# Expert weights' parts 2 and 3 read during the mixer's last chunk, into a buffer shared by both phases

## The chip, the core and the metric

The kernel runs on one core of a Trainium2 chip. The metric is the device time of one execution in microseconds (us). The engines are named as in the profile: PE (TensorE matmuls), PEld (its weight loads), DVE (VectorE), ACT (ScalarE), POOL (GpSimd) and SP (SyncE). SPq, ACTq and POOLq are the queues from which these engines issue DMA transfers.

## What is computed

One layer over 2048 tokens of width 1024: a mixer of three parallel branches with an output projection, then a mixture of 16 experts (4 groups of 4, two experts per token), then a final norm, all in float32.

```python
def reference(x, ...):
    mix = hybrid_mixer(h, ...)                  # z = rmsnorm(x) @ W_in, branches A, B, C, then @ w_out
    h = h + mix
    ffn = hierarchical_moe(rms_norm(h, norm_ffn_g[l]), ...)
    h = h + ffn
    return rms_norm(h, final_norm_g)

def expert_block(args):                         # inside hierarchical_moe, for a block of sorted tokens
    xb, e = args
    return (jax.nn.silu(xb @ w_gate[e]) * (xb @ w_up[e])) @ w_down[e]
```

## The kernel before

**First phase (`phases12`).** The mixer's projections are cut into 22 chunks of weight columns, 14 of `w_in` and 8 of `w_out`, numbered n = 0 to 21. Generators that run a step per tick of a small scheduler (`Flow`) read a chunk's float32 weights, split them on ACT and DVE into a high and a low part, and keep them in a tile `w`. The pool of that tile has two buffers, used in turn, so chunk n takes the buffer of chunk n-2. The last loop goes over `h` (two halves of 1024 tokens), `m` (four chunks of `w_out`) and `t` (eight tiles of 128 tokens). With `m == 3` each finished tile is written to two DRAM tensors, `hd` and `hc`, and squared on ACT for the norm. A generator `route` then selects experts, sorts the tokens and writes tables; between its halves it reads the first two parts of the experts' weights into two buffers `stg` of the pool `c8`.

**Second phase (`moe`).** The experts' weights come in 96 parts of 1 MB, six an expert: u = 0 to 3 are gate and up columns, u = 4 and 5 are rows of the down projection. Part n is read by two DMAs of 512 KB into a staging place `raw(n)`, and DVE splits it into the ring slot n % 9: first the high half (L1600, or L1598 for a down part), then the low half (L1618, L1616). ACT does some of the splitting of parts 0 and 1. DVE counts finished parts in the semaphore `s_w`. Parts 0 and 1 are staged in the two `stg` buffers, parts 2 to 5 in ring slots that are still unused (6 and 7), and from part 6 on the two `stg` buffers are used in turn: SP issues part n (n > 7) only when part n-2 has been split (L1567). The slots are reused when PE has done the last block of the expert that they held.

PE takes blocks of 128 tokens, sorted by expert. For block b it does the gate and up products in two halves of two groups of 12 or more matmuls (`gu`, L1692), each group waiting for its part by `s_w`, and the down product of the block before (`down`, L1731 to L1733). ACT applies the activation (`glu`), POOL multiplies (`hm`), gathers tokens, scatters results back, and scales finished rows by the final norm's gains `gf`.

What the steps touch, in lines that words don't say:

```python
                    for n in range(NST, 96):
                        if n == 4:
                            sp.wait_ge(p_q, 2)
                        if n >= 6:
                            sp.wait_ge(s_w, n - NST + 1 if n > 7 else n - 5)
...
        raw = lambda n: ring[:, 6 + (n - 2) // 2, n % 2].bitcast(F32) if 2 <= n < 6 else stg[n % NST]
```

Of the kernel before, what the change touches and what calls it, by code (L numbers as in the profile page):

```python
# [9 lines left out]
F32 = mybir.dt.float32  # L10
F32R = mybir.dt.float32r
BF = mybir.dt.bfloat16
I32 = mybir.dt.int32
# [4 lines left out]
DRAM = bass.MemoryType.DRAM  # L18

P = 128  # L20
S = 2048
D = 1024
# [74 lines left out]
NST = 2  # L97
# [44 lines left out]
        self.until(lambda: not self.g)  # L142


def phases12(tc, io, hd, hc, tab, gcol, ident, c8, stg):


    nc = tc.nc
# [2 lines left out]
    with ctx:  # L151
# [3 lines left out]
        lg = tab[:, 0:320].rearrange("p (t n) -> p t n", n=20)  # L155
        base = pool("base")
        small = pool("small", 2)
        wp = pool("w", 2)
        rawp = pool("raw", 2)
        uvp = pool("uvp")  # L160
        psz = pool("psz", 4, space=PSUM)
# [39 lines left out]
        def wgen():  # L201
            for n in range(len(chunks)):
                raws = load_w_raw(n)
                yield
                while begun[0] < n - 1:
                    yield
                w = wp.tile([P, 2, 8, 276], F32R, name="w")
                for k in range(0, 8, 2):
                    rw_ = raws[k // 4][:, k % 4:k % 4 + 2, :]
                    for j in range(2):  # L210
                        g = col(chunks[n][2], k + j)
                        A.activation(w[:, 0, k + j, 0:256], rw_[:, j], AF.Copy, scale=g)  # L212
                    for j in range(2):
                        stt(w[:, 1, k + j, 0:256], rw_[:, j], col(chunks[n][2], k + j), w[:, 0, k + j, 0:256].bitcast(F32), OP.mult, OP.subtract)
                    yield
                if n in routed:
                    while "rw" not in done:
                        yield
                    G.tensor_copy(w[:, 0, :, 256:276], routed[n])
                    tt(w[:, 1, :, 256:276], routed[n], w[:, 0, :, 256:276].bitcast(F32), OP.subtract, G)  # L220
                wt[n] = w
                if 6 <= n < 14:
                    yield from route_w(n - 6)
                if n == 2:
                    yield from spatial_w()
            done.add("w")
# [859 lines left out]
        def route():  # L1086
# [237 lines left out]
            for k in range(2):  # L1324
                G.iota(digit[:, k], pattern=[[1, 16], [0, 48]], base=1 + 32 * k, channel_multiplier=0, allow_small_or_imprecise_dtypes=True)
            digits(slice(0, 8))
            while stg is not None and len(stg) < NST:
                t = c8.tile([P, 2048], F32, name="stg", tag="c8")
                for o, i in stage(io, t, len(stg)):
                    nc.sync.dma_start(out=o, in_=i)  # L1330
                stg.append(t)
            yield from half(1)

            acc = bank(psm, "m")[:, 0:96]
# [105 lines left out]
        for h in range(2):  # L1440
            F.until(lambda: ("r", h) in done)
            for m in range(4):
                w = chunk(n)
                n += 1
                if h == 0 and m == 1:
                    F.add(pipeline([(lambda p=p: yprep(p), lambda: ("a", 1) in done) for p in range(4, 8)]))
                for t in range(8):
                    F.until(lambda: ("y", h * 8 + t) in done and h * 8 + t in ht)
                    N = 276 if m == 3 else 256
                    za, zc = bank(psz, "z"), bank(psz, "z")  # L1450
                    dst = [za[:, 0:N], (bank(psm, "m")[:, 0:N] if m == 3 else za[:, 256:512]), zc[:, 0:N]]
                    for j, ks in enumerate(((0, 1, 2), (3, 4, 5), (6, 7))):
                        for k in ks:
                            split3(nc, dst[j], [xT[:, s, k, t * P:(t + 1) * P] for s in range(2)],
                                   [w[:, s, k, 0:N] for s in range(2)], k == ks[0], k == ks[-1])
                    x = ht[h * 8 + t][:, m * 256:(m + 1) * 256]
                    for j in range(3):
                        r = rsd[:, j, h * 8 + t:h * 8 + t + 1]
                        stt(x, dst[j][:, 0:256], r, x, OP.mult, OP.add)
                        if m == 3:  # L1460
                            l = lg[:, h * 8 + t, :]
                            stt(l, dst[j][:, 256:276], r, l, OP.mult, OP.add)
                    F.tick()
                    g = h * 8 + t
                    whole = g < 12
                    if m == 2 and not whole:
                        p2_sq(g, (0, 768), False)
                        if t == 7:
                            ts(hss[3][:, 0], hss[3][:, 0], 1.0 / D, EPS, OP.mult, OP.add)
                    if m == 3:  # L1470
                        p2_sq(g, (0 if whole else 768, D), True)
                        if t % 4 == 3 or h == 1 and t == 1:
                            F.add(p2_post(list(range(g - (1 if h == 1 and t < 4 else 3), g + 1)), whole))
                        done.add(("yfree", 8 + t))
# [20 lines left out]
def moe(tc, io, hd, hc, out, tab, gcol, ident, stg):  # L1495
# [5 lines left out]
    with ctx:  # L1501
        E = ctx.enter_context
        mp = E(tc.tile_pool(name="moe", bufs=1))
        pp = E(tc.tile_pool(name="mps", bufs=1, space=PSUM))
        ring = mp.tile([P, RING, 2, 2048], F32R, name="ring")
        xg = mp.tile([P, 2, D + 16], F32, name="xg")
        sc = mp.tile([P, 48, 2], F32, name="sc")
        xs = mp.tile([P, 2, 2, 8, P], F32R, name="xs")
        hs = mp.tile([P, 512], F32, name="hs")
        hu = mp.tile([P, 512], F32, name="hu")  # L1510
        hh = mp.tile([P, 2, 4, P], F32R, name="hh")
        yb = mp.tile([P, 2, D], F32, name="yb")
        gf = mp.tile([P, D], F32, name="gf")
        idf = mp.tile([P, 48], I32, name="idf")
        nw = mp.tile([P, 12], F32, name="nw")
        jb = hu[:, 0:256].bitcast(mybir.dt.float8e4)
        nid = mp.tile([P, P], F32R, name="nid")
        s0, vh, nt, c15, gl, ceps, cmag = (nw[:, i:i + 1] for i in range(7))
        ya = nw[:, 8:10]
        ew = mp.tile([P, 6, 2], F32, name="ew")  # L1520
        es, et, ev, ey = ew[:, 0:2], ew[:, 2], ew[:, 3], ew[:, 4:6]
        pg = [pp.tile([P, 512], F32, name="pg%d" % i) for i in range(2)]
        pt = [pp.tile([P, 4, P], F32, name="pt%d" % i) for i in range(2)]
# [3 lines left out]
        S_ = lambda n: tc.alloc_semaphore(n)  # L1527
        s_st = [S_("st%d" % i) for i in range(NST)]
        s_w, s_hi, s_ha, p_q, p_c = S_("w"), S_("hi"), S_("ha"), S_("pq"), S_("pc")
        s_er = [S_("er%d" % i) for i in range(4)]  # L1530

        raw = lambda n: ring[:, 6 + (n - 2) // 2, n % 2].bitcast(F32) if 2 <= n < 6 else stg[n % NST]
        s_u = [S_("u%d" % i) for i in range(6)]
        s_hm, s_hT, s_T, s_hlo, s_d0 = (S_(n) for n in ("hm", "hT", "T", "hlo", "d0"))
        s_Tl, s_hl, a_xh, a_hh, a_sc, p_k = (S_(n) for n in ("Tl", "hl", "axh", "ahh", "asc", "pk"))
# [22 lines left out]
        with tc.tile_critical():  # L1558
            with nc.Block() as blk:
                @blk.sync  # L1560
                def _(sp):
                    sp.wait_ge(p_q, 1)
                    for n in range(NST, 96):
                        if n == 4:
                            sp.wait_ge(p_q, 2)
                        if n >= 6:
                            sp.wait_ge(s_w, n - NST + 1 if n > 7 else n - 5)  # L1567
                        if n == RING:
                            sp.dma_start(out=gf, in_=io["final_norm_g"].unsqueeze(0).to_broadcast((P, D))).then_inc(s_gf, 16)
                        for o, i in stage(io, raw(n), n):  # L1570
                            sp.dma_start(out=o, in_=i).then_inc(s_er[n - 2] if n < 6 else s_st[n % NST], 16)

                @blk.vector
                def _(v):
                    nhi = nha = 0
                    for n in range(96):
# [4 lines left out]
                            v.wait_ge(s_u[u], c)  # L1581
                        if n >= 6:
                            v.wait_ge(s_st[j], 32 * ((n - 6) // NST + 1))
                        elif n >= NST:
                            v.wait_ge(s_er[n - 2], 32)
                        src = raw(n)
                        r = n % RING
                        q = n % 6
# [191 lines left out]
                def _(a):  # L1780
# [28 lines left out]
                    def glu(b, f):  # L1809
                        a.wait_ge(s_u[2 * f + 1], b + 1)  # L1810
                        if f == 0:
                            a.wait_ge(a_sc, 2 * b + 2)
                        a.activation(hs[:, f * 256:(f + 1) * 256], pg[f][:, 0:256], AF.Silu, scale=sc[:, b, 0:1])
                        a.activation(hu[:, f * 256:(f + 1) * 256], pg[f][:, 256:512], AF.Copy, scale=sc[:, b, 0:1]).then_inc(a_g[f], 1)  # L1814

# [57 lines left out]
                    evx(0)  # L1873
                    scale(0)
                    evxl(0)
                    if 3 in AH:
                        a.wait_ge(s_er[1], 32)
                        hi(3, range(4))
                    chain(a, nb, 0, NBMAX, step)
                    n = 0  # L1880
                    for i in (1, 0):
# [81 lines left out]

def trunk(tc, io, out):
    nc = tc.nc
    with tc.tile_pool(name="outer", bufs=1) as po, tc.tile_pool(name="c8", bufs=2) as c8, tc.tile_pool(name="odr", bufs=1, space=DRAM) as pd:
        tab = po.tile([P, 368], F32, name="tab")
        gcol = po.tile([P, 8], F32, name="gcol")
        ident = po.tile([P, P], F32, name="ident")
        make_identity(nc, ident)  # L1970
        hd = pd.tile([S + P, D], F32, name="hd")
        hc = pd.tile([S, D + 16], F32, name="hc")
        stg = []
        phases12(tc, io, hd, hc, tab, gcol, ident, c8, stg)
        moe(tc, io, hd, hc, out, tab, gcol, ident, stg)


# [23 lines left out]
```

## Time and profile before

| | before |
|---|---|
| median of 3 runs | 1590.1 us (1586.15 to 1593.86) |
| the profiled execution, its time | 1590.12 us |
| its span, first to last instruction | 1588.3 us |
| mean granted TensorE clock | 0.966 |
| PE busy | 94% |
| DVE, ACT, POOL busy | 61%, 54%, 31% |
| HBM | 217.09 MB read, 76.94 MB written |

The share of busy time is a mean over the whole span. The first phase ends and the second begins at about 762 us; what one stage is limited by has to be read in that stage. Times in the rows below are counted from the span's start.

### The profile page before, as it was taken

To read this page: it belongs to the slowest core of one execution; us is meant where nothing else is said; L and a number is where in the kernel's file an instruction comes from. 1 tells how busy PE (TensorE), PEld (TensorE's weight loads), DVE (VectorE), ACT (ScalarE), POOL (GpSimd) and SP (SyncE) were. 2 spreads that over 40 slices of the span, in tenths; PEclk is the share of its full clock that TensorE was granted. 3 is DMA by queue.
4 is the path that set the end of the run, shared out by engine and by line. 5 is a ranking of instruction groups with operands and counts; after the bars stand their busy time and mean duration, and the time that the engine had idled before them with its cause. 6 is when DMAs were issued, how large, how long until landed. Compare 5 with 4: busy or idle time off the path is not lost.

```text
span 1588.3 us, 25588 instructions
## 1 busy us (share of the span) xinstructions
PE 1489.4 (94%) x8373; PEld 1283.5 (81%) x8374; DVE 976.4 (61%) x2009; ACT 865.6 (54%) x1915; POOL 484.6 (31%) x400
## 2 busy tenths in 40 slices
PE   7998989999999999996899899999999999999993
PEld 6776888878899989996688678888888888888882
DVE  6588752664642678888888876577888858203001
ACT  6368544687454444311346456665666665666662
POOL 0132000000000000010355545655555555455442
PEclk9999988999999999998899999999999999999996
DMA  6247733213633627607678887778888877434342
GB/s 179 69 80 142 208 104 120 93 54 93 188 99 104 236 81 263 241 27 267 215 226 241 259 253 198 214 214 264 272 222 236 261 220 204 126 75 107 90 116 74
DMA packets 212862, 267.46 MB, mean 168 GB/s; under 512 B 34808, under 2 KB 177344, under 8 KB 212736
## 3 DMA queue, kind: packets, MB, share of 16 engines
q1 hardware_dynamic: 187792, 201.95, 40.3%
q0 software_dynamic: 24672, 62.80, 16.3%
q8 instruction: 78, 1.28, 0.3%
q10 hardware_dynamic: 272, 1.05, 0.2%
q14 instruction: 48, 0.39, 0.1%
HBM read 217.09 MB, written 76.94 MB: 185 GB/s over the span
## 4 chain that ended last, share of the span: by engine, by line
PE 74%; DVE 13%; DMA 4%; ACT 4%; issue 2%; POOL 1%; SPq 0%; DVEq 0%; POOLq 0%; ACTq 0%
PE pg L1692 24%; PE z L90 8%; PE z L92 8%; PE z L91 8%; PE pd L1733 4%; PE pd L1732 4%; PE pd L1731 4%; DMA stg<-in_expert_w_up_dram 3%; DVE ring L1600 2%; PE pt L1699 2%; DVE ring L1618 2%; DVE ht L171 1%; DVE w L171 1%; PE m L924 1%; DVE xT L169 1%
## 5 line engine op out<-in xcount | busy, mean ns | idle before, releaser
L1692 PE MATMUL pg<-ring,xs 128*128 x2016 | 488.3, 395 | 9.7 <-DVE ring L1618 8.0
L1692 PEld LDWEIGHTS pg<-ring,xs 128*128 128x128 f32 x2016 | 378.2, 189 | 89.7 <-issue 11.8
L90 PE MATMUL z<-w,xT 128*128 128x256 f32 (+1 forms) x848 | 250.4, 295 | 5.6 <-DVE ht L171 3.8
L92 PE MATMUL z<-w,xT 128*128 128x256 f32 (+1 forms) x848 | 244.9, 289 | 6.9 <-DVE xT L169 6.9
L91 PE MATMUL z<-w,xT 128*128 128x256 f32 (+1 forms) x848 | 244.6, 288 | 0.0
L1600 DVE TENSOR_SCALAR ring<-stg,gcol 128x512 fp32r<-128x512 f32 x242 | 130.9, 602 | 169.8 <-PE pg L1692 86.7
L1618 DVE SCALAR_TENSOR_TENSOR ring<-stg,gcol,ring 128x512 fp32r<-128x512 f32 x248 | 213.9, 923 | 0.0
L90 PEld LDWEIGHTS z<-w,xT 128*128 128x128 f32 x848 | 164.3, 194 | 9.0 <-issue 5.1
L92 PEld LDWEIGHTS z<-w,xT 128*128 128x128 f32 x848 | 164.1, 194 | 8.2 <-DVE xT L169 8.2
L91 PEld LDWEIGHTS z<-w,xT 128*128 128x128 f32 x848 | 164.5, 194 | 1.4 <-issue 1.4
L1731 PE MATMUL pd<-ring,hh 128*128 x336 | 131.4, 391 | 1.7 <-DVE hh L1637 1.7
L1896 POOL DMA_INDIRECT hd<-yb,tab x41 | 77.5, 1891 | 177.8 <-ACT yb L1835 177.8
L1733 PE MATMUL pd<-ring,hh 128*128 x336 | 131.2, 390 | 0.0
L1732 PE MATMUL pd<-ring,hh 128*128 x336 | 131.2, 390 | 0.0
L1910 POOL TENSOR_TENSOR hs<-hs,hu 128x256 f32<-128x256 f32 x84 | 106.5, 1268 | 50.1 <-ACT hu L1814 47.8
L1945 POOL TENSOR_TENSOR yb<-yb,gf 128x1024 f32<-128x1024 f32 x40 | 116.2, 2905 | 4.7 <-ACT hu L1860 4.7
L171 DVE SCALAR_TENSOR_TENSOR w<-raw,vec,w 128x256 fp32r<-128x256 f32 x176 | 82.0, 510 | 55.4 <-ACT w L212 55.4
L212 ACT ACTIVATE w<-raw,vec 128x256 fp32r<-128x256 f32 x176 | 77.1, 497 | 60.8 <-PE z L92 36.7
L90 PE MATMUL z<-xT,w 128*128 128x512 f32 x256 | 109.8, 429 | 0.2 <-ACT xT L312 0.2
L171 DVE SCALAR_TENSOR_TENSOR ht<-z,rsd,ht 128x256 f32<-128x256 f32 x176 | 85.1, 484 | 30.1 <-PE z L92 22.2
L91 PE MATMUL z<-xT,w 128*128 128x512 f32 x256 | 101.5, 396 | 0.2 <-DVE xT L169 0.2
L92 PE MATMUL z<-xT,w 128*128 128x512 f32 x256 | 101.3, 396 | 0.0
(441 smaller groups left out, 2573.2 us busy)
## 6 DMA issues: line engine op xcount, KB each, us to landing
stg<-in_expert_w_gate_dram SPq DMA_DIRECT2D x62, 512.0 KB
stg<-in_expert_w_up_dram SPq DMA_DIRECT2D x62, 512.0 KB
stg<-in_expert_w_down_dram SPq DMA_DIRECT2D x60, 512.0 KB
raw<-in_w_in_dram SPq DMA_DIRECT2D x48, 256.0 KB
raw<-in_w_out_dram SPq DMA_DIRECT2D x24, 512.0 KB
ht<-in_x_dram SPq DMA_DIRECT2D x16, 512.0 KB
yp<-yTd SPq DMA_DIRECT2D x8, 1024.0 KB
hd<-ht SPq DMA_DIRECT2D x16, 512.0 KB
```

Source lines behind the costliest of these rows:

```text
L90: nc.tensor.matmul(ps, ah, bh, start=first, stop=False)
L91: nc.tensor.matmul(ps, ah, bl, start=False, stop=False)
L92: nc.tensor.matmul(ps, al, bh, start=False, stop=last)
L171: stt = lambda o, a, s, b, o0, o1: V.scalar_tensor_tensor(out=o, in0=a, scalar=s, in1=b, op0=o0, op1=o1)
L1600: x = v.tensor_scalar(out=ring[:, r, 0, sl], in0=src[:, sl], scalar1=g, scalar2=None, op0=OP.mult)
L1618: x = v.scalar_tensor_tensor(out=ring[:, r, 1, sl], in0=src[:, sl], scalar=g, in1=hi, op0=OP.mult, op1=OP.subtract)
L1692: i = t.matmul(pg[f], xx[j // 2], w[j % 2], start=k == 0 and j == 0, stop=k == 7 and j == 2)
L1731: t.matmul(pd[n], hh[:, 0, kf], w[0], start=kf == 0, stop=False)
L1732: t.matmul(pd[n], hh[:, 0, kf], w[1], start=False, stop=False)
L1733: i = t.matmul(pd[n], hh[:, 1, kf], w[0], start=False, stop=kf == 3)
L1910: g.tensor_tensor(out=o, in0=o, in1=hu[:, f * 256:(f + 1) * 256], op=OP.mult).then_inc(s_hm, 1)
L1945: g.tensor_tensor(out=z, in0=z, in1=gf, op=OP.mult).then_inc(p_z, 1)
```

## The change

Chunks with an even n take their `w` tile from a new pool `we` of one buffer, which both phases see; odd chunks take it from the old pool, which now has one buffer. Chunk 20 is the last in `we`. When chunk 21 begins (`h == 1`, `m == 3`), ACT issues the reads of parts 2 and 3 into that buffer (`early`). In the second phase parts 4 and 5 alone are staged in the ring (slot 7), and SP issues them without the wait for `p_q` 2. Several small tiles of the second phase (`yb`, `gf`, `hs`, `hu`, `sc`, `idf`, `nw`, `ew`) are now cuts of `early`: `yb`, `gf`, `hs` and `hu` lie where parts 2 and 3 are staged, the others behind them. Before its first write of `hs`, ACT waits until four parts have been split. A branch that was never taken (`3 in AH`) is removed.

```diff
-                w = wp.tile([P, 2, 8, 276], F32R, name="w")
+                w = (wp if n % 2 else we).tile([P, 2, 8, 276], F32R, name="w")
...
-            while stg is not None and len(stg) < NST:
+            for n in range(NST):
                 t = c8.tile([P, 2048], F32, name="stg", tag="c8")
...
+                if h == 1 and m == 3:
+
+                    t = we.tile([P, 4416], F32, name="w", tag="w")
+                    for j in range(2):
+                        for o, i in stage(io, t[:, j * 2048:(j + 1) * 2048], 2 + j):
+                            A.dma_start(out=o, in_=i)
+                    stg.append(t)
...
+        early = stg[NST]
...
+        yb = cut(2 * D).rearrange("p (a n) -> p a n", a=2)
+        gf = cut(D)
+        hs, hu = cut(512), cut(512)
...
+        raw = lambda n: early[:, (n - 2) * 2048:(n - 1) * 2048] if 2 <= n < 4 else ring[:, 7, n % 2].bitcast(F32) if 4 <= n < 6 else stg[n % NST]
...
                     sp.wait_ge(p_q, 1)
-                    for n in range(NST, 96):
-                        if n == 4:
-                            sp.wait_ge(p_q, 2)
+                    for n in range(4, 96):
                         if n >= 6:
                             sp.wait_ge(s_w, n - NST + 1 if n > 7 else n - 5)
...
+                        if b == 0 and f == 0:
+                            a.wait_ge(s_w, 4)
```

On ACT the four reads stand in the first phase between the squares of chunk 20's last four tiles (128x768) and those of chunk 21's first four (128x1024); this is the piece of the difference there:

```order
 L212 ACTIVATE w<-raw,vec 128x256 x8
 L1065 ACTIVATE junk,hss<-ht 128x768 x4
+L1450 DMA w<-in_expert_w_gate_dram 128x4x256
+L1450 DMA w<-in_expert_w_up_dram 128x4x256
+L1450 DMA w<-in_expert_w_gate_dram 128x4x256
+L1450 DMA w<-in_expert_w_up_dram 128x4x256
 L1065 ACTIVATE junk,hss<-ht 128x1024 x4
 L1065 ACTIVATE junk,hss<-ht 128x256 x4
```

Nothing else moves on ACT there; the squares stand behind four issues more.

On SP the second phase began with parts 2 and 3 (gate, up), then parts 4 and 5 (down) behind a second wait for `pq`, then part 6 behind `w`, the count of split parts (the kernel before):

```order
L1571 DMA ring<-in_expert_w_gate_dram 128x4x256 [waits pq]
L1571 DMA ring<-in_expert_w_up_dram 128x4x256
L1571 DMA ring<-in_expert_w_gate_dram 128x4x256
L1571 DMA ring<-in_expert_w_up_dram 128x4x256
L1571 DMA ring<-in_expert_w_down_dram 128x1024 [waits pq]
L1571 DMA ring<-in_expert_w_down_dram 128x1024 x3
L1571 DMA stg<-in_expert_w_gate_dram 128x4x256 [waits w]
L1571 DMA stg<-in_expert_w_up_dram 128x4x256
```

The changed kernel begins there with the down parts:

```order
L1582 DMA ring<-in_expert_w_down_dram 128x1024 [waits pq]
L1582 DMA ring<-in_expert_w_down_dram 128x1024 x3
L1582 DMA stg<-in_expert_w_gate_dram 128x4x256 [waits w]
L1582 DMA stg<-in_expert_w_up_dram 128x4x256
L1582 DMA stg<-in_expert_w_gate_dram 128x4x256 [waits w]
```

Four reads have gone from the queue's head, and every part behind them stands two parts earlier.

On DVE the start of the second phase was this (before; `er0` and `er1` are the arrivals of parts 2 and 3, `er2` that of part 4):

```order
L1618 SCALAR_TENSOR_TENSOR ring<-stg,gcol,ring 128x512 [waits ha] x6
L1600 TENSOR_SCALAR ring<-ring,gcol 128x512 [waits er0]
L1600 TENSOR_SCALAR ring<-ring,gcol 128x512 x3
L1618 SCALAR_TENSOR_TENSOR ring<-ring,gcol 128x512 [waits hi] x4
L1600 TENSOR_SCALAR ring<-ring,gcol 128x512 [waits er1]
L1600 TENSOR_SCALAR ring<-ring,gcol 128x512 x3
L1618 SCALAR_TENSOR_TENSOR ring<-ring,gcol 128x512 [waits hi] x4
L1598 CAST ring<-ring 128x1024 [waits er2]
```

In the changed kernel (`w` is the shared buffer, and `er0` is now part 4):

```order
L1629 SCALAR_TENSOR_TENSOR ring<-stg,gcol,ring 128x512 [waits ha] x6
L1611 TENSOR_SCALAR ring<-w,gcol 128x512 x4
L1629 SCALAR_TENSOR_TENSOR ring<-w,gcol,ring 128x512 [waits hi] x4
L1611 TENSOR_SCALAR ring<-w,gcol 128x512 x4
L1629 SCALAR_TENSOR_TENSOR ring<-w,gcol,ring 128x512 [waits hi] x4
L1609 CAST ring<-ring 128x1024 [waits er0]
```

The waits for the arrival of parts 2 and 3 are gone from DVE; the operations and their order are the same.

## Rows read from the trace of the kernel before

**Rows 1.** Chain that ended last, 760 to 1000 us: start, length, what.
```profile
765.29 7.77 DMA ring<-in_expert_w_up_dram
773.08 1.67 DVE ring L1600 x4
...
920.39 3.03 PE pg L1692 x12
```

**Rows 2.** PE's waits, 760 us to the end: total us, times, longest.
```profile
PE pg L1692 <- DVE ring L1618: 8.0, 3, 4.1
```

**Rows 3.** PE's waits, 921 us to the end, the whole list.
```profile
PE ph L1699 <- issue: 3.4, 1, 3.4
PE pd L1731 <- DVE hh L1637: 1.7, 1, 1.7
```

**Rows 4.** Timeline of PE: start, length, what, and in brackets idle before.
```profile
879.94 5.61 PE L1692 MATMUL pg<-ring,xs 128*128 x24
...
890.14 2.88 PE L1692 MATMUL pg<-ring,xs 128*128 x12
...
898.08 0.39 PE L1733 MATMUL pd<-ring,hh 128*128 x1
902.52 4.60 PE L1692 MATMUL pg<-ring,xs 128*128 x12 [4.05 <-DVE ring L1618]
909.22 4.60 PE L1692 MATMUL pg<-ring,xs 128*128 x12 [2.09 <-DVE ring L1618]
...
920.39 3.03 PE L1692 MATMUL pg<-ring,xs 128*128 x12 [1.84 <-DVE ring L1618]
```

**Rows 5.** Windows: PE, PEld, DVE, ACT, POOL busy, PE clock, DMA share, GB/s.
```profile
902.40:907.00 4.60, 4.48 (x12) 3.31 (x12) 2.94 (x6) 4.16 (x11) 2.37 (x1) 0.63 1.03 252
```

**Rows 6.** Timeline of DVE.
```profile
722.74 0.16 DVE L170 TENSOR_SCALAR hss<-hss 128x2 f32<-128x2 f32 x1
...
763.62 5.44 DVE L1618 SCALAR_TENSOR_TENSOR ring<-stg,gcol,ring 128x512 fp32r<-128x512 f32 x8
773.08 1.67 DVE L1600 TENSOR_SCALAR ring<-ring,gcol 128x512 fp32r<-128x512 f32 x4 [4.02 <-DMA ring<-in_expert_w_up_dram]
...
786.24 2.35 DVE L1616 TENSOR_TENSOR ring<-ring 128x1024 fp32r<-128x1024 f32 x2
...
806.87 5.30 DVE L1600 TENSOR_SCALAR ring<-stg,gcol 128x512 fp32r<-128x512 f32 x4 [2.09 <-DMA stg<-in_expert_w_up_dram]
```

**Rows 7.** DVE's waits for staged parts, 760 to 921 us; none names a ring slot.
```profile
DVE ring L1600 <- DMA stg<-in_expert_w_up_dram: 18.5, 12, 2.7
DVE ring L1598 <- DMA stg<-in_expert_w_down_dram: 4.2, 3, 1.5
```

**Rows 8.** Timeline of POOL.
```profile
807.29 3.42 POOL L1930 TENSOR_SCALAR gf<-gf 128x1024 f32<-128x1024 f32 x1
...
826.03 2.95 POOL L1945 TENSOR_TENSOR yb<-yb,gf 128x1024 f32<-128x1024 f32 x1
```

**Rows 9.** Timeline of SP's queue: DMA issues.
```profile
764.85 0.39 SPq L1571 DMA_DIRECT2D ring<-in_expert_w_gate_dram  x1
...
772.75 1.77 SPq L1571 DMA_DIRECT2D ring<-in_expert_w_down_dram  x4
...
775.84 3.14 SPq L1571 DMA_DIRECT2D stg<-in_expert_w_gate_dram  x1
...
794.30 0.37 SPq L1571 DMA_DIRECT2D stg<-in_expert_w_gate_dram  x1
```

**Rows 10.** Timeline of ACT.
```profile
716.83 1.06 ACT L1065 ACTIVATE junk<-ht 128x1024 bf16<-128x1024 f32 x1 [1.86 <-DVE ht L171]
...
781.47 0.48 ACT L1813 ACTIVATE hs<-pg,sc 128x256 f32<-128x256 f32 x1
```

**Rows 11.** Timeline of ACT's queue, its one DMA issue.
```profile
28.89 0.45 ACTq L318 DMA_DIRECT2D xp<-in_x_dram  x1
```

**Rows 12.** Windows, columns as in rows 5.
```profile
748.00:752.00 4.00, 0.46 (x3) 0.08 (x2) 3.63 (x18) 0.21 (x1) 1.59 (x5) 0.50 0.01 3
```

More of the change, by code (lines that the diff above doesn't have):

```diff
@@ L142, in drain, with phases12 @@
         self.until(lambda: not self.g)
-def phases12(tc, io, hd, hc, tab, gcol, ident, c8, stg):
+def phases12(tc, io, hd, hc, tab, gcol, ident, c8, we, stg):
     nc = tc.nc
@@ L157, in phases12 @@
         small = pool("small", 2)
-        wp = pool("w", 2)
+        wp = pool("w")
         rawp = pool("raw", 2)
@@ L1326, in route @@
             digits(slice(0, 8))
-            while stg is not None and len(stg) < NST:
+            for n in range(NST):
                 t = c8.tile([P, 2048], F32, name="stg", tag="c8")
-                for o, i in stage(io, t, len(stg)):
+                for o, i in stage(io, t, n):
                     nc.sync.dma_start(out=o, in_=i)
-                stg.append(t)
+                stg.insert(n, t)
             yield from half(1)
@@ L1505, in moe, with cut @@
         ring = mp.tile([P, RING, 2, 2048], F32R, name="ring")
+        early = stg[NST]
+        off = [0]
+        def cut(n):
+            off[0] += n
+            return early[:, off[0] - n:off[0]]
         xg = mp.tile([P, 2, D + 16], F32, name="xg")
-        sc = mp.tile([P, 48, 2], F32, name="sc")
         xs = mp.tile([P, 2, 2, 8, P], F32R, name="xs")
-        hs = mp.tile([P, 512], F32, name="hs")
-        hu = mp.tile([P, 512], F32, name="hu")
+        yb = cut(2 * D).rearrange("p (a n) -> p a n", a=2)
+        gf = cut(D)
+        hs, hu = cut(512), cut(512)
         hh = mp.tile([P, 2, 4, P], F32R, name="hh")
[L1512 to L1515, printed above, removed]
+        sc = cut(96).rearrange("p (b j) -> p b j", j=2)
+        idf = cut(48).bitcast(I32)
+        nw = cut(12)
         jb = hu[:, 0:256].bitcast(mybir.dt.float8e4)
@@ L1519, in moe @@
         ya = nw[:, 8:10]
-        ew = mp.tile([P, 6, 2], F32, name="ew")
+        ew = cut(12).rearrange("p (a b) -> p a b", b=2)
         es, et, ev, ey = ew[:, 0:2], ew[:, 2], ew[:, 3], ew[:, 4:6]
@@ L1529, in moe @@
         s_w, s_hi, s_ha, p_q, p_c = S_("w"), S_("hi"), S_("ha"), S_("pq"), S_("pc")
-        s_er = [S_("er%d" % i) for i in range(4)]
-        raw = lambda n: ring[:, 6 + (n - 2) // 2, n % 2].bitcast(F32) if 2 <= n < 6 else stg[n % NST]
+        s_er = [S_("er%d" % i) for i in range(2)]
+        raw = lambda n: early[:, (n - 2) * 2048:(n - 1) * 2048] if 2 <= n < 4 else ring[:, 7, n % 2].bitcast(F32) if 4 <= n < 6 else stg[n % NST]
         s_u = [S_("u%d" % i) for i in range(6)]
@@ L1570, in _ @@
                         for o, i in stage(io, raw(n), n):
-                            sp.dma_start(out=o, in_=i).then_inc(s_er[n - 2] if n < 6 else s_st[n % NST], 16)
+                            sp.dma_start(out=o, in_=i).then_inc(s_er[n - 4] if n < 6 else s_st[n % NST], 16)
                 @blk.vector
@@ L1583, in _ @@
                             v.wait_ge(s_st[j], 32 * ((n - 6) // NST + 1))
-                        elif n >= NST:
-                            v.wait_ge(s_er[n - 2], 32)
+                        elif n >= 4:
+                            v.wait_ge(s_er[n - 4], 32)
                         src = raw(n)
@@ L1875, in _ @@
                     evxl(0)
-                    if 3 in AH:
-                        a.wait_ge(s_er[1], 32)
-                        hi(3, range(4))
                     chain(a, nb, 0, NBMAX, step)
@@ L1965, in trunk @@
     nc = tc.nc
-    with tc.tile_pool(name="outer", bufs=1) as po, tc.tile_pool(name="c8", bufs=2) as c8, tc.tile_pool(name="odr", bufs=1, space=DRAM) as pd:
+    with tc.tile_pool(name="outer", bufs=1) as po, tc.tile_pool(name="c8", bufs=2) as c8, tc.tile_pool(name="we", bufs=1) as we, tc.tile_pool(name="odr", bufs=1, space=DRAM) as pd:
         tab = po.tile([P, 368], F32, name="tab")
@@ L1973, in trunk @@
         stg = []
-        phases12(tc, io, hd, hc, tab, gcol, ident, c8, stg)
+        phases12(tc, io, hd, hc, tab, gcol, ident, c8, we, stg)
         moe(tc, io, hd, hc, out, tab, gcol, ident, stg)
```

## The prediction

> **What bounds the kernel now.** I read the page first: PE is busy for 94% of a span of 1588.3 us, so a gain has to come from the few places where PE has nothing to do. The list of what PE waited for over the second phase names one that has to do with weights: three waits of 8.0 us in total for DVE's low halves [rows 2]. After 921 us PE waits only twice, both times in the tail [rows 3]; from there on its own matmuls set the time. The timeline places the three waits in one block, the first of expert 4, where weights arrive later than PE does: before the groups at 902.52, 909.22 and 920.39 [rows 4]. What stands behind them is in the chain that ended last: from 765.29 to 920.39 it runs through DMA and DVE alone and never through PE [rows 1]. It begins with the read of parts 2 and 3, for which DVE sat idle 4.02 us at 773.08 [rows 6], and goes on through a loop of two staging buffers: SP issues part 8 at 794.30, as soon as part 6 is split [rows 9], the data lands, DVE splits it, SP issues part 10. DVE's waits up to 921 us are all for DMA, 15 of them with 22.7 us, none for a ring slot held by PE [rows 7]. So each microsecond by which this loop starts earlier should reach 920.39, and from there the end.
>
> **What the cover allows.** How much can be gained before PE itself is the limit? In block 6, with its weights there, the last gate-and-up group begins at 890.14, 10.20 us after the block's first at 879.94 [rows 4]. PE is free for block 7 at 898.08 + 0.39 = 898.47. Undisturbed, that block's last group would begin at 908.67 rather than 920.39. The cap is 11.7 us: the 8.0 of waits, and 3.7 that PE ran slower. That is seen in the groups at 902.52 and 909.22, which take 4.60 us against 2.88 for such a group in block 6 [rows 4]; the granted clock there is 0.63, between the levels of 1.2 and 2.4 GHz, behind the first wait [rows 5]. Whether the clock falls again after the change doesn't matter below the cap, since the arrival of the last part sets the time of the last group.
>
> **The parts of the change.**
>
> *The wait that goes.* ACT and DVE finish parts 0 and 1 at 763.62 + 5.44 = 769.06. Parts 2 to 5 were split from 773.08 to 786.24 + 2.35 = 788.59, in 15.5 us without a gap [rows 6]. With parts 2 and 3 in the buffer they begin at 769.06 and end at 784.6: 4.0 us earlier. This holds only if the parts behind arrive in time. Parts 4 and 5 take the place in SP's queue that parts 2 and 3 had (764.85, rows 9), whose data came 7.77 us after its issue at 765.29 [rows 1]; they land at about 773.1 and are wanted after two parts of the 15.5 us, at about 777. Parts 6 and 7 follow at once, since parts 0 and 1 are split by 769.06; before they stood behind the wait for `p_q` and two parts more, and the second pair of their four reads began at 775.84 [rows 9]. At the pace of 7.8 us for 2 MB they are there at 781, wanted at 784.6. So the loop begins 4.0 us earlier, and part 8's issue moves from 794.30 to about 790.3.
>
> *What the loop makes of it.* The splits' lengths depend on POOL. Part 9's high half, four operations, took 5.30 us at 806.87, against 1.67 at 773.08 [rows 6]; POOL's scaling of `gf` lay on it with 3.42 us at 807.29 [rows 8]. POOL follows PE's blocks, which don't move before 898, while DVE's splits move by 4 us, so such meetings fall differently. If part 9 is split before the scaling begins, its 3.6 us come off one buffer's branch of the loop, and part 10 is likely to meet the scaling instead. If a split meets a multiply of `yb` that it missed before, 2.95 us go on [rows 8]. The bounds are +3.6 and -2.95; I take +1.0, because the one stretch known to lie on the chain is longer than a multiply, and the scaling happens once.
>
> The Trainium skill, page "SBUF — State Buffer", section "Who interferes with whom", says that DVE and GpSimd share one port pair as a lock, and that the later of two such operations blocks for the other's whole length. The trace agrees: 5.30 - 1.67 = 3.63 against 3.42. By that rule the meetings are whole operations and cannot be shared out, so that the head start is carried, enlarged or eaten in steps; eaten, it is the second rival below.
>
> *The four issues on ACT.* They stand where ACT is idle for 1.86 us before its square at 716.83 [rows 10]. One issue on that queue took 0.45 us [rows 11]; four are 1.8 us. Below nothing there is no gain to be had, since nothing that ACT delivers there is late. The nearest dear row is an issue of 3.14 us on SP at 775.84 with the queue full [rows 9]. I take 0.45, as the row is ACT's own and DMA is nearly idle then; the cost on the path is 0. The other end is the slower rival.
>
> *The 2 MB themselves.* They push the stores of `hd` and `hc` back by what 2 MB cost, at the dearest 7.8 us [rows 1]. The DMA engines have emptied before 748 to 752 us, with a share of 0.01 there [rows 12], and the second phase begins at 762. Even pushed by 7.8 us the last store is done at about 756; cost 0. Without this cover it would be 7.8.
>
> *The new wait and the shared tiles.* ACT now waits for four split parts before its first activation of `hs`, which ran at 781.47 [rows 10]; part 3 will be split at about 769.06 + 8.5 = 777.6. Behind it on ACT stand the activations and copies for PE's next block, with 3.9 us to spare; cost 0. The first writes of `yb` and `gf` lie behind the first down product and part 7. The split into pools `w` and `we` leaves chunk n with the buffer of chunk n-2; cost 0.
>
> *Sum.* 4.0 + 1.0 = 5.0 us, below the cap of 11.7. The profiled execution took 1590.12 us, the same as the median of the runs shown, so I predict 1585.1 us.
>
> **The rivals.**
>
> *The loop gains more than it was given.* DMA is busy for most of this stretch (share 1.03 at 252 GB/s in rows 5), and 2 MB leave it. If transport and not the sequence of split and read is what limits, the gain is what 2 MB cost, 7.8 us [rows 1], and with a meeting saved (3.6) the cap: 11.7. Time 1578.4 to 1582.3. Against it: DVE's waits are short, 1.5 us in the mean [rows 7], as a loop of read, split, read leaves them. Chance 0.15.
>
> *The head start is eaten on the way.* One or two multiplies of 2.95 us [rows 8] meet splits that they missed before: gain 4.0 - 2.95 = 1.0, or a loss of 1.9. Time 1589.1 to 1592. For it: the meetings move, as said. Against it: they are as likely to leave the chain as to enter it. Chance 0.2.
>
> *Slower: the issues hold up ACT.* DVE takes up the squares of chunk 21's first two tiles at 722.74 [rows 6], and ACT needs 2 x 1.06 us for these [rows 10], plus reading the sums. ACT is free at 714.97, so the four issues may take about 5.3 us, 1.3 each; beyond that DVE's in-order queue stands still, PE's results aren't taken up, and the phase ends later by the excess. Above 2.6 us each it outweighs the gain; at 3.14 each it is 12.6 - 5.3 = 7.3 us against 5.0, so 1592.4. For more than 0.5% it would take twice that. Chance 0.06.
>
> That the change doesn't do what it says is excluded by the order of instructions: DVE's waits for parts 2 and 3 are gone.
>
> **How the numbers follow.** The forecast, a gain of 4 to 6.5 us, has a chance of 0.59, with a range of its own of 1583.6 to 1586.1. A measurement of this kernel can tell about 0.5%, 8 us, from no change (the runs shown spread by that). The range reaches over most of the first rival and of the second, 1580 to 1591.5, and leaves out the gain near the cap and the slower case. Faster by over 0.5% means below 1582.1: nearly all of the first rival, 0.13. Slower by over 0.5% is left 0.04, for the slower rival with a dearer price than any row has. The rest, 0.83, is within 0.5%.
>
> **What the profile after should show.** DVE's idle of 4.02 us before part 2 gone, and parts 2 to 5 split by about 784.6; the four reads issued on ACT's queue at about 715 in under 2.5 us; SP's first issue of the second phase at about 765 a down part; part 8 issued at about 790; PE's waits for weights 3 to 4.5 us rather than 8.0, the last group of block 7 at about 915.4; nothing new in what PE waits for after that. The prediction is wrong if DVE waits for parts 4 to 7 instead, if its splits of parts 8 to 27 take as much longer as they begin earlier, or if the second phase begins later than 762.

## The result, and the profile after

| | before | after |
|---|---|---|
| median, beside each other | 1589.8 us (6 runs, 1586.15 to 1593.86) | 1598.67 us (6 runs, 1596.82 to 1607.93) |
| ratio to before, 95% interval | | 1.0064 [1.0045, 1.0083] |
| the profiled execution, its span | 1590.12 us, 1588.3 us | 1596.82 us, 1595.1 us |
| PE busy | 1489.4 us | 1502.9 us |

The changed kernel is slower by some 10 us (0.64% of 1590), where 5 us less was predicted; it lies outside the predicted range. The waits that were meant to go did go. These are PE's waits from 760 us to the end in the changed kernel (total us, times, longest), and below the dots its whole list after 921 us:

```profile
PE pg L1703 <- DVE ring L1629: 2.7, 2, 2.4
...
PE ph L1710 <- issue: 3.3, 1, 3.3
PE pd L1742 <- DVE hh L1648: 1.7, 1, 1.7
```

The wait for weights fell from 8.0 to 2.7 us [rows 2], and behind 921 us stand the same two waits as before [rows 3]. DVE's timeline at the start of the second phase:

```profile
761.42 5.45 DVE L1629 SCALAR_TENSOR_TENSOR ring<-stg,gcol,ring 128x512 fp32r<-128x512 f32 x8
766.79 1.66 DVE L1611 TENSOR_SCALAR ring<-w,gcol 128x512 fp32r<-128x512 f32 x4
...
779.94 2.35 DVE L1627 TENSOR_TENSOR ring<-ring 128x1024 fp32r<-128x1024 f32 x2
```

Part 2 follows part 1 without the 4.02 us of [rows 6], and four parts take 15.5 us as before. The reads on ACT's queue, and the square that stands behind them:

```profile
711.92 0.38 ACTq L1450 DMA_DIRECT2D w<-in_expert_w_gate_dram  x1
712.35 0.52 ACTq L1450 DMA_DIRECT2D w<-in_expert_w_up_dram  x1
...
712.91 0.52 ACTq L1450 DMA_DIRECT2D w<-in_expert_w_gate_dram  x1
713.46 0.53 ACTq L1450 DMA_DIRECT2D w<-in_expert_w_up_dram  x1
714.62 1.06 ACT L1065 ACTIVATE junk<-ht 128x1024 bf16<-128x1024 f32 x1 [1.86 <-DVE ht L171]
```

Its idle time of 1.86 us, which ended with DVE's `ht`, is to the digit that of [rows 10]: the issues cost nothing. SP's queue begins with the down parts, and part 8 follows at 787.52 (794.30 in rows 9):

```profile
762.65 2.04 SPq L1582 DMA_DIRECT2D ring<-in_expert_w_down_dram  x4
...
787.52 0.37 SPq L1582 DMA_DIRECT2D stg<-in_expert_w_gate_dram  x1
```

In the block that used to stand still, PE's timeline has one wait left, and the last group begins at 912.30 rather than 920.39 [rows 4]:

```profile
906.97 4.59 PE L1703 MATMUL pg<-ring,xs 128*128 x12 [2.36 <-DVE ring L1629]
912.30 3.05 PE L1703 MATMUL pg<-ring,xs 128*128 x12
```

Of these 8.1 us, 2.2 are the earlier start of splitting. DVE has a wait that the kernel before does not have [rows 7]. It is for PE's last down product, that is for a ring slot that PE still uses (760 to 921 us; total, times, longest):

```profile
DVE ring L1611 <- PE pd L1744: 8.3, 3, 4.2
```

And the chain that ended last, which ran through DMA and DVE up to 920.39 [rows 1], now runs through PE from 766 us until it crosses to DVE at 895.76, behind the third of these waits:

```profile
888.73 2.79 PE pg L1703 x12
...
895.76 1.68 DVE ring L1611 x4
```

So at 912 us the changed kernel is 8 us ahead, and at the end it is 7 us behind, with no new wait of PE in between. What is left is the work itself. The view of the tile `ph` gives the pace: the lines below are one of the two reads of `ph` that ACT makes in each block, 27 of them between 1000 and 1500 us, where PE never waits. Columns are the shortest, median and longest duration in ns, then the first and last start. The kernel before:

```profile
L1819 ACT ACTIVATE hh<-ph x27: 567/578/584, 1008.4 to 1485.7; 128x512 fp32r<-128x512 f32 x27
```

And the changed kernel:

```profile
L1832 ACT ACTIVATE hh<-ph x27: 572/577/582, 1002.2 to 1490.7; 128x512 fp32r<-128x512 f32 x27
```

26 blocks took 477.3 us and now take 488.5: 18.36 us a block against 18.79. Over 42 blocks the 0.43 us are 18 us. They lie in the matmuls with the ring as moving operand (48 of `pg` and 24 of `pd` a block, so some 6 ns each). In the chain that ended last (start, length, what), the kernel before has groups of 2.72 us for 12 matmuls:

```profile
1453.07 2.72 PE pg L1692 x12
```

The changed kernel:

```profile
1452.99 0.87 PE pt L1710 x8
1453.86 2.79 PE pg L1703 x12
```

The transposes beside them, eight in 0.87 us, take as long as before; the chain of the kernel before has:

```profile
1540.54 0.87 PE pt L1699 x8
```

The window from 1400 to 1500 us has PE busy throughout at a granted clock of 1.00 (the number behind POOL's), first in the changed kernel:

```profile
1400.00:1500.00 100.00, 100.00 (x463) 81.61 (x462) 14.53 (x16) 60.11 (x137) 49.57 (x38) 1.00 0.37 86
```

And in the kernel before:

```profile
1400.00:1500.00 100.00, 100.00 (x473) 83.54 (x472) 14.56 (x16) 60.91 (x137) 49.51 (x38) 1.00 0.38 91
```

DVE, ACT, POOL and the DMA engines are as busy in one as in the other, so no load of theirs tells the two apart. The instructions of PE and their order are the same. What differs is where the tiles lie. The pool `we` stands ahead of the second phase's pool and takes 17664 bytes of each partition, so the ring moved from 34912 to 52576 bytes, `xs` (the stationary operand of `pg`) from 191072 to 208352, `hh` (that of `pd`) from 211552 to 224736. These are the addresses in the built programs. Each piece of the ring, of `xs` and of `hh` that a matmul reads begins a multiple of 512 bytes behind its tile's first byte, so the remainder of the distance by 256 is the same for all these matmuls.

### The profile page after: what moved, and what is told of

It is laid out like the page before. It is cut to its first block, busy times and chain, and to the rows that moved or that the text cites. A ratio compares the mean times of both kernels' runs of the same rounds, so it can differ in the third digit from the quotient of the medians.

```text
span 1595.1 us, 25590 instructions
## 1 busy us (share of the span) xinstructions
PE 1502.9 (94%) x8373; PEld 1281.0 (80%) x8374; DVE 977.7 (61%) x2009; ACT 865.8 (54%) x1915; POOL 465.7 (29%) x400
## 4 chain that ended last, share of the span: by engine, by line
PE 83%; DVE 8%; ACT 4%; issue 2%; DMA 1%; POOL 1%; SPq 0%; POOLq 0%; DVEq 0%; ACTq 0%
PE pg L1703 29%; PE z L90 8%; PE z L92 8%; PE z L91 8%; PE pd L1744 5%; PE pd L1743 5%; PE pd L1742 5%; PE pt L1710 2%; PE pt L1715 1%; DVE w L171 1%; DVE ht L171 1%; PE ph L1710 1%; DVE xT L169 1%; PE m L924 1%; PE m L864 1%
## 5 line engine op out<-in xcount | busy, mean ns | idle before, releaser
L1703 PE MATMUL pg<-ring,xs 128*128 x2016 | 496.9, 398 | 4.4 <-DVE ring L1629 2.7
L1611 DVE TENSOR_SCALAR ring<-stg,gcol 128x512 fp32r<-128x512 f32 x242 | 127.5, 587 | 181.5 <-PE pg L1703 93.5
L1629 DVE SCALAR_TENSOR_TENSOR ring<-stg,gcol,ring 128x512 fp32r<-128x512 f32 x248 | 209.9, 906 | 0.0
L1742 PE MATMUL pd<-ring,hh 128*128 x336 | 133.8, 398 | 1.7 <-DVE hh L1648 1.7
L1743 PE MATMUL pd<-ring,hh 128*128 x336 | 133.4, 397 | 0.0
L1744 PE MATMUL pd<-ring,hh 128*128 x336 | 133.4, 397 | 0.0
L1906 POOL DMA_INDIRECT hd<-w,tab x41 | 74.6, 1819 | 191.9 <-ACT w L1848 191.9
L1955 POOL TENSOR_TENSOR w<-w 128x1024 f32<-128x1024 f32 x40 | 116.8, 2921 | 0.6 <-ACT w L1873 0.6
L1920 POOL TENSOR_TENSOR w<-w 128x256 f32<-128x256 f32 x84 | 94.0, 1119 | 50.2 <-ACT w L1827 49.3
```

The costliest lines, as they stand in the source:

```text
L1611: x = v.tensor_scalar(out=ring[:, r, 0, sl], in0=src[:, sl], scalar1=g, scalar2=None, op0=OP.mult)
L1629: x = v.scalar_tensor_tensor(out=ring[:, r, 1, sl], in0=src[:, sl], scalar=g, in1=hi, op0=OP.mult, op1=OP.subtract)
L1703: i = t.matmul(pg[f], xx[j // 2], w[j % 2], start=k == 0 and j == 0, stop=k == 7 and j == 2)
L1742: t.matmul(pd[n], hh[:, 0, kf], w[0], start=kf == 0, stop=False)
L1743: t.matmul(pd[n], hh[:, 0, kf], w[1], start=False, stop=False)
L1744: i = t.matmul(pd[n], hh[:, 1, kf], w[0], start=False, stop=kf == 3)
```

## The experiments

**The theory and its rivals.** Theory: the place of the operands sets the pace of a matmul. It could be the ring's own address (A), or that of the stationary operands against it (B). Rival (C): something else of the change, above all the tiles that now share a buffer.

**Moving the tiles of the kernel before by 256 and 512 bytes.** An unused tile goes ahead of the ring or behind it, with 64 floats for 256 bytes, 128 for 512:

```diff
+        mp.tile([P, 64], F32, name="gap")
         ring = mp.tile([P, RING, 2, 2048], F32R, name="ring")
```

> The kernel before, with 256 unused bytes a partition put ahead of the ring, so that the ring's first byte moves from 34912 to 35168 (from 96 to 352 in steps of 512, where it also stands in the changed kernel) and every tile behind it moves by 256 too. Nothing else differs. Theory A (where the ring, the 512-column moving operand, stands sets the time of a matmul): the pg and pd matmuls go from one in about 226.7 ns to one in about 233.3 ns, some 0.43 us more in each of 42 blocks, so 1590 + 18 = about 1608 us. Rival B (the place of the stationary operands xs and hh against the ring's does it): their distance to the ring is kept, so 1590. Rival C (not a place, but the tiles that now share one buffer, or the order of events): 1590.

> The kernel before, with 256 unused bytes a partition put behind the ring: the ring stays at 34912, and xg, xs, hh and what follows move by 256 bytes. Theory A (the ring's own place): 1590 us, no change, pg groups of 24 stay near 5.44 us. Rival B (the stationary operands' place, or their distance to the ring): slower, up to 1608 us. Rival C (neither): 1590.

> The kernel before, with 512 unused bytes a partition put ahead of the ring: ring at 35424, again 96 in steps of 512, but 608 in steps of 1024. Theory A with a period of 512 bytes or less: 1590 us. Theory A with a longer period, or with the absolute place mattering: about 1608 us. Rivals B and C: 1590.

Measured beside a median of 1591.19 us, 10 runs each: 1591.78 with 256 ahead (ratio 0.9999 [0.9982, 1.0016]), 1589.97 with 256 behind (0.9994 [0.998, 1.0008]), 1592.15 with 512 ahead (1.001 [0.9994, 1.0027]). None is slow. A, as the ring's address in steps of 512, is out; the three fit C, B with other distances, and A with a period longer than 1024.

**The changed kernel with `xg` ahead of the ring.** Same instructions, same addresses of `xs` and `hh`:

```diff
+        xg = mp.tile([P, 2, D + 16], F32, name="xg")
         ring = mp.tile([P, RING, 2, 2048], F32R, name="ring")
+        xs = mp.tile([P, 2, 2, 8, P], F32R, name="xs")
+        hh = mp.tile([P, 2, 4, P], F32R, name="hh")
```

> The changed kernel with xg allocated ahead of the ring, and xs and hh right behind it: xs and hh keep the addresses that they have in the changed kernel, the ring moves from 52576 to 60896 (from 352 to 480 in steps of 512). Theory A: the time moves if 480 is another kind of place than 352; if it is as good as the 96 of before, the 18 us go and the gain stays, 1598.7 - 18 = about 1580 us; if it is as bad, 1598.7. Rival B: the distance of xs and hh to the ring changes by 128, so it may move as well. Rival C: 1598.7.

1588.82 us (10 runs), ratio 0.998 [0.996, 1.0001]: 10 us less than the changed kernel. Its blocks, in the view of `ph`:

```profile
L1832 ACT ACTIVATE hh<-ph x27: 574/578/583, 1004.1 to 1481.7; 128x512 fp32r<-128x512 f32 x27
```

477.6 us for 26 blocks is the pace of before. Only the ring and `xg` moved, so C falls; A and B stay. The time fell by less than the 18 us expected: by the ratios 0.84%, 13 us, with intervals of some 3 us either way on both. What the change is worth at the quick pace is measured below, where a wait of PE that takes part of the rest is shown, too.

**The ring's address or the distance.** In the five quick kernels so far the distance from the ring to `xs` and to `hh` is a multiple of 256 bytes, in the changed kernel it is 128 more than one. Four kernels set these against each other. Two have the tiles of the kernel before in another order, which puts the ring at 52576:

```diff
+        xg = mp.tile([P, 2, D + 16], F32, name="xg")
+        yb = mp.tile([P, 2, D], F32, name="yb")
+        nid = mp.tile([P, P], F32R, name="nid")
+        sc = mp.tile([P, 48, 2], F32, name="sc")
+        mp.tile([P, 64], F32, name="gap")
         ring = mp.tile([P, RING, 2, 2048], F32R, name="ring")
...
         gf = mp.tile([P, D], F32, name="gf")
+        mp.tile([P, 32], F32, name="gapb")
+        xs = mp.tile([P, 2, 2, 8, P], F32R, name="xs")
+        hh = mp.tile([P, 2, 4, P], F32R, name="hh")
```

The second of them is without `gapb`. The third is the kernel before with 128 unused bytes behind the ring, the fourth the changed kernel with `xs` and `hh` right behind the ring and `xg` behind these.

> The kernel before with none of the change's reads, but with ring, xs and hh at the addresses of the changed kernel (52576, 208352, 224736), by another order of the same tiles and 384 unused bytes. If the place of these operands is all that slowed the changed kernel's matmuls, a block takes 18.8 us instead of 18.36 and the time is about 1591 + 18 = 1609 us. If it is the shared buffer, or the reads, or anything else of the change: 1591.

> As the kernel before with the ring at 52576, where it stands in the changed kernel, but xs and hh 128 bytes further down than there (208224, 224608), so that their distance to the ring is a multiple of 512 bytes, as in the kernel before. If the ring's own address decides: about 1609 us, blocks of 18.8 us. If the distance from the ring to the stationary operands decides (128 over a multiple of 256 in the changed kernel, 0 or 256 over a multiple of 512 in the five others so far, all quick): 1591 us, blocks of 18.36.

> The kernel before with 128 unused bytes behind the ring: the ring stays at 34912, the distance of xs and hh to it becomes 128 over a multiple of 512, as in the changed kernel. Distance theory: about 1609 us, blocks of 18.8 us. Theory of the ring's own address: 1591 us.

> The changed kernel with xs and hh right behind the ring and xg behind them: the ring stays at 52576, the distance of xs and hh to it becomes a multiple of 512 bytes. Distance theory: the matmuls are quick again, about 1588.8 us as with xg first, blocks of 18.36. Theory of the ring's own address: 1598.7 us, blocks of 18.8.

Beside a median of 1590.33 us, with 4 runs of each slow kernel and 10 of each quick one: 1607.11 with all operands as in the changed kernel (1.0099 [1.0076, 1.0122]), 1591.67 with the ring there but the distance a multiple of 256 (1.001 [0.9995, 1.0025]), 1608.28 with the ring unmoved and 128 bytes behind it (1.0113 [1.0097, 1.013]), 1590.89 for the changed kernel with `xg` last (0.9997 [0.9977, 1.0018]). The kernel with 128 bytes behind the ring, whose ring stands where it always stood, has these blocks:

```profile
L1820 ACT ACTIVATE hh<-ph x27: 568/578/583, 1009.6 to 1498.2; 128x512 fp32r<-128x512 f32 x27
```

And the one with the ring at 52576 and the even distance:

```profile
L1820 ACT ACTIVATE hh<-ph x27: 568/577/583, 1008.9 to 1487.4; 128x512 fp32r<-128x512 f32 x27
```

18.79 us a block in the one, 18.40 in the other: in these kernels the pace follows the distance (B) and not the ring's address, in both directions and in both kernels. Nor is it the address of `xs` and `hh` by itself: with `xg` first these two stand where the changed kernel has them, and the blocks are quick. The distances of `xs` and of `hh` had the same remainder in each kernel, so the two are not told apart. 128 unused bytes in a kernel without any of the change's reads or shared tiles cost 18 us.

**A distance of 64.** Two kernels, with 64 unused bytes behind the ring, and with 64 ahead of it and 64 behind:

> The kernel before with 64 unused bytes behind the ring: the ring at 34912, xs and hh at a distance of 64 over a multiple of 512. If every distance that is no multiple of 256 is slow: blocks of 18.8 us and about 1608 us. If only a distance near 128 over a multiple of 256 is slow: blocks of 18.36 us and 1591 us. If the cost follows whether ring and xs start in the same 128-byte half of 256 bytes (here 96 and 160: not the same): slow as well, which the next kernel tells apart.

> The kernel before with 64 unused bytes ahead of the ring and 64 behind it: the same distance of 64 as the kernel with 64 behind alone, but ring (160 over a multiple of 256) and xs (224) both start in the upper 128 bytes of 256. If the distance alone decides, the same block time as with 64 behind alone. If the half in which each starts decides: quick, 18.36 us, where the other is slow.

1607.65 and 1605.29 us, two runs each, beside 1589.38 (1.0114 [1.0081, 1.0146] and 1.0099 [1.0067, 1.0131]). Both are slow, so in which half of 256 bytes an operand starts is not what counts. All twelve placements together; the block time is worked out as above, from the first and last read of `ph` between 1000 and 1500 us:

| distance of `xs` and `hh` to the ring | kernels | us a block |
|---|---|---|
| a multiple of 256 | before, 256 ahead, 512 ahead, 256 behind, ring at 52576, `xg` first, `xg` last | 18.36 to 18.45 |
| 64 more | 64 behind, 64 on both sides | 18.81, 18.82 |
| 128 more | after, all as after, 128 behind | 18.79 |

**What the early reads are worth at the quick pace.** The changed kernel with `xg` first again, and the same kernel with the early reads taken out:

```diff
-                    for j in range(2):
-                        for o, i in stage(io, t[:, j * 2048:(j + 1) * 2048], 2 + j):
-                            A.dma_start(out=o, in_=i)
...
-                    for n in range(4, 96):
+                    for n in range(2, 96):
```

> The same kernel as a_xg_first (the changed kernel with the ring where its matmuls are quick), in more rounds, beside the kernel before. My sum of the prediction (stall for part 2 gone, 4.0 us, and 1.0 us of the split's meetings) gives 1591 - 5 = 1586 us; the two runs so far gave 2.4 us less and 0.6 us more than before. If the head start is given back by later waits or by lower clocks: 1589 to 1591.

> The changed kernel with xg first, and the early reads taken out: parts 2 and 3 are read by SP at the start of the second phase, into the same shared buffer; addresses, pools and all else stay. If the early reads are worth what they move (the stall at part 2): slower than a_xg_first by 4 to 6 us, about 1592 to 1594. If the rest of the change (the shared buffer, parts 4 and 5 no longer waiting) brings the gain: the same as a_xg_first.

With the reads 1584.57 us (12 runs, 0.9971 [0.9953, 0.999]), without them 1589.32 (12 runs, 0.9999 [0.9987, 1.001]), before 1589.38. The reads alone bring 4.75 us by these medians, and the shared buffer, taken alone, nothing; the first run with `xg` first and the run with `xg` last gave less (2.4 us, and a loss of 0.6). The gain is not there in each execution: of the 12 runs with the reads seven took 1580.68 to 1584.61 us, five 1586.52 to 1592.96. One of the latter was profiled, and in it PE waited for weights as long as before:

```profile
PE pg L1703 <- DVE ring L1629: 8.6, 4, 4.8
```

DVE's timeline in that execution:

```profile
764.48 0.88 DVE L1611 TENSOR_SCALAR ring<-stg,gcol 128x512 fp32r<-128x512 f32 x2 [0.85 <-SPq L1571]
...
798.53 1.74 DVE L1611 TENSOR_SCALAR ring<-stg,gcol 128x512 fp32r<-128x512 f32 x4 [2.51 <-DMA stg<-in_expert_w_up_dram]
...
806.88 5.34 DVE L1611 TENSOR_SCALAR ring<-stg,gcol 128x512 fp32r<-128x512 f32 x4 [3.47 <-DMA stg<-in_expert_w_up_dram]
```

And in the one that was profiled of the first run of the same kernel (1586.09 us):

```profile
760.30 0.88 DVE L1611 TENSOR_SCALAR ring<-stg,gcol 128x512 fp32r<-128x512 f32 x2 [0.85 <-SPq L1571]
...
799.29 1.67 DVE L1611 TENSOR_SCALAR ring<-stg,gcol 128x512 fp32r<-128x512 f32 x4 [2.66 <-DMA stg<-in_expert_w_up_dram]
```

The kernel before began at 762.82. Where the splitting began at 764.48, two waits for arriving parts ate what was left of the lead: part 9's last read took 9.88 us, 6.84 before, so that it is split from 806.88 on, as before at 806.87 [rows 6], and its high half takes 5.34 us. Where it began at 760.30, part 9 is split from 799.29 on, in 1.67 us. The second phase's start varies so without the change, too: the first split began at 760.00 to 765.86 in the kernel before and the eight made from it above.

In the execution that began at 760.30, too, part of the lead was lost. Part 8 was issued at 786.25, 8 us earlier than before, but the last group of block 7 began at 916.10, 4.3 us earlier. PE waited for a multiply of POOL's, and DVE for ring slots that PE still used (total, times, longest):

```profile
PE ph L1710 <- POOL w L1920: 6.0, 1, 6.0
DVE ring L1611 <- PE pd L1744: 11.5, 3, 6.3
```

Ahead of that multiply POOL had its third gather of tokens:

```profile
768.22 15.46 POOL L1902 DMA_INDIRECT xg<-hc,tab  x1 [3.21 <-ACT w L1812]
```

It took 13.92 us in the execution that began at 764.48, 1.48 in the changed kernel, 0.99 in the kernel before. Why it is long in some executions with the early reads, no run here shows.

## Why the prediction was wrong

**The step that failed** is the one on the new wait and the shared tiles, which put the tiles' new places at nothing: "The split into pools `w` and `we` leaves chunk n with the buffer of chunk n-2; cost 0." It looked at the order of the buffers' use and took the place of a tile for free. The pool `we` pushed the ring 17664 bytes further, which by itself costs nothing (1.001 [0.9995, 1.0025] above). What cost time is that `sc`, 384 bytes, went from between the ring and `xs`: the distance fell from 156160 to 155776 bytes, from 610 times 256 to 128 over 608 times 256. (From between `xs` and `hh` went `hs` and `hu`, 4096 bytes, which leaves `hh` the same remainder.) That cost 0.99% [0.76, 1.22] when done alone in the kernel before (all as after), some 16 us. With the gain of the reads off it, 0.5 to 4.6 us by the three ratios below, 11 to 15 us are left; the changed kernel lost 10, with an interval of 7 to 13.

**The stall for part 2, 4.0 us:** right. It went [rows 6], four parts took 15.5 us, and part 8 was issued earlier, by 6.8 us in the profiled executions, of which 2.2 are the earlier start of splitting (761.42 for 763.62).

**"So each microsecond by which this loop starts earlier should reach 920.39":** true in the changed kernel (6.8 us at part 8, 8.1 at the last group), not in the two profiled executions with `xg` first (8 us became 4.3, and 3.4 became 1.3). It rested on DVE never waiting for a ring slot. With the parts there earlier DVE did wait for slots, 8.3 us in the changed kernel and 11.5 in the first of those two.

**The gain of 5.0 us:** not settled. Three comparisons at the quick pace gave medians 4.8 us lower, 2.4 lower and 0.6 higher than before, with ratios 0.9971, 0.998 and 0.9997. A gain of 5.0 would be 0.9969, which the first two intervals hold and the third, [0.9977, 1.0018], does not; the mean of the three is some 3 us. The share of 1.0 us for the meetings with POOL can't be told apart, though one meeting moved as was said: in the changed kernel part 9's high half took 1.68 us rather than 5.30, and part 10's low half 4.34 rather than 2.35.

**The four issues on ACT, 0:** right; 0.38 to 0.53 us each, for which 0.45 was taken. The slower rival, which needed 2.6 us each, did not occur. The kernel got slower by a mechanism that was not among the rivals.

**The head start eaten:** seen, in part or whole, in both profiled executions with `xg` first. In one the arrival of parts 8 and 9 ate it, in the other POOL's late multiply and the ring slots; the second rival had named POOL's multiplies that lengthen a split. The 5.34 us against 1.67 are the meeting with POOL's scaling again, as [rows 6, 8] had it; here the scaling took 3.41 us at 807.74. The Trainium skill, page "SBUF — State Buffer", section "Who interferes with whom", says that where a DVE and a GpSimd operation both need the port pair that they share, the first has it for the whole instruction and the other is fully blocked; the difference, 3.67 us, agrees with the 3.41.

**What would have made the prediction wrong** was listed as waits of DVE for parts 4 to 7, longer splits, or a late second phase. None of these made the changed kernel slower; that PE's own matmuls could change their pace was not in the list, since PE's instructions were the same.

## What to carry to other kernels

A change that allocates a buffer or takes tiles out of a pool moves every tile behind it, so what it costs is known only when the pace of the main loop in a stretch without waits (us a block, ns a matmul) has been compared in both kernels. Where PE is 94% busy, 6 ns a matmul outweigh a stall that was removed. Here it took an order of tiles in which the distance from moving to stationary operand is a multiple of 256 bytes: the changed kernel with `xg` ahead of the ring is the quickest of those tried, at 0.9971 [0.9953, 0.999] of before in one comparison and 0.998 [0.996, 1.0001] in the other.

## What the hardware showed unexpectedly

The float32r matmuls of 512 columns that have the ring as moving operand run at a pace that depends on the distance between their two operands in a partition: groups of 12 take 2.72 us with a distance that is a multiple of 256 bytes (2.73 to 2.78 in some places, above all behind the transposes), 2.79 to 2.81 us with 64 or 128 more, at granted clock 1.00, in each of the placements tried.

A second pair of operands agrees in part. The two matmuls `pt` at L1715 have `nid`, a negated identity matrix, as stationary and `xs` as moving operand. With `xg` first their distance is 80 times 256 bytes, and the chain of that kernel has:

```profile
1301.62 0.45 PE pt L1715 x2
```

With `xg` last it is 128 over 112 times 256, and the chain has them slower, beside a quick group of `pg`:

```profile
1301.55 0.47 PE pt L1715 x2
1302.01 2.73 PE pg L1703 x12
```

But in the changed kernel the distance of this pair is 80 times 256, as with `xg` first, and its chain has them slow as well, between matmuls that are slow:

```profile
1456.88 0.47 PE pt L1715 x2
```

So either what runs beside a matmul counts, too, or such a row takes in a part of its neighbours' time; no run tells these apart. The Trainium skill, page "SBUF — State Buffer", section "Operand start alignment", asks that an operand start at a multiple of its element size, and calls this a rule of legality, not of speed; each place tried here keeps it, and speed turned out to have a condition of its own. What in the chip causes it, and what distances other than 0, 64 and 128 do to it (modulo 256), no run here shows.
